# Weight sums of the seven-product blocks: two of four moved from accumulating transfers to VectorE, with shared constant tiles, more raw buffers and new scheduler numbers

## The chip, the core and the metric

The kernel runs on one NeuronCore of a Trainium2 chip. TensorE (PE; its weight loads are listed as PEld), VectorE (DVE), ScalarE (ACT), GpSimd (POOL) and SyncE (SP) each take their instructions in program order and wait for one another through semaphores. SP issues the plain DMA transfers; POOL issues the transfers that add to what lies at their destination. The metric is the device time of one execution in microseconds (us).

## The reference, cut to what matters

Two layers on a residual stream x of 256 tokens by 1024 channels, all float32. Each layer is

```
x += 1/2 * postnorm(SwiGLU(prenorm(x)))        # first feed-forward network (FFN)
x += postnorm(mixer(prenorm(x)))               # S5 state space model + chunk attention, gated
x += 1/2 * postnorm(SwiGLU(prenorm(x)))        # second FFN
def swiglu(h, w_gate, w_up, w_down):
    return (jax.nn.silu(h @ w_gate) * (h @ w_up)) @ w_down     # 1024 -> 2816 -> 1024
```

The S5 part discretises a diagonal complex system with a handful of constant tables that depend on the layer alone (read-out matrices, rotations, decays); the scan over 64-step chunks uses them for both halves of the tokens.

## The kernel before

**Tiles.** The tokens are two tiles t of 128 rows. All weights lie in one array `wall` of 368 chunks of 128 x 1024 float32 (512 KB); a layer has 66 chunks for each FFN and 52 for the mixer, so the FFNs begin at chunks 0, 118, 184 and 302. A chunk is loaded into a buffer of the class `raw`, rounded by ACT to the short matmul format (`wh`, L468), and DVE takes the remainder `raw - wh` (`wl`, L469). With the activations split in the same way, a product of a token tile with half a chunk is three matmuls of 128 x 512 columns: high by high, high by low, low by high (`mm_two_k`, L490, `wide_step`, L508).

**Blocks.** The 2816 hidden columns of an FFN are six blocks b = 0 to 5. Blocks 1 and 3 (`SEVEN`, L31; eight blocks in all) are computed by `seven` (L636): gate and up weights of the block, over two halves of the inner dimension and for two token tiles, are multiplied with seven products in place of eight. A block has twelve chunks i to i+11. Its four weight quadrants are two chunks each: quadrant 11 is i and i+1, quadrant 21 is i+3 and i+4, quadrant 12 is i+5 and i+6, quadrant 22 is i+7 and i+8; i+2, i+9, i+10 and i+11 belong to the down projection of the block before. Products w1 and w2 use quadrants 11 and 21 as they are; w5, w6, w7, w4 use sums of quadrants; w3 uses quadrant 22. The sums are made in place in the `raw` buffers, and each is then converted again by ACT and DVE. `sums` (L610) makes the matching sums of the activations, once for each FFN.

**The four weight sums.** `minus` (L650) negates quadrants 21 and 12 on ACT, and `add` (L654) issues, through `add_to` (L378), an accumulating transfer from POOL for each of the two buffers: 12 into 11 (for w5), 22 into 12 (for w7), 22 into 11 (for w6), 11 into 21 (for w4). That is eight transfers for a block, 64 in all.

**Order.** `Graph` records the operations with a cost, a due time that `take` (L482) and `prod` (L680) derive from `TAU` (L41) times the place in the program, and margins by stream (`MARGIN`, L42). `schedule` (L207) then plays the program with these costs, takes on each engine the operation that can start first (the earliest due among those), and hands out the buffers of `SLOTS` (L37). Each engine's instructions are emitted in the order that comes out. A transfer issued by POOL counts as landed `ADD_LAT` (L54) after its issue. Every matmul, conversion and sum therefore stands in a fixed queue: an instruction that waits holds up all that stand behind it on its engine.

**Constants of S5.** `persistent` (L765) makes `CT`, `D0`, `mt`, `E` (and the two halves of `BT`, L906) in memory of their own, for the whole program; `prep` (L777) fills them once for each layer.

Most instructions of a kind share the line of the helper that records them: L369 is every ACT operation, L376 every DVE tensor-tensor operation, L416 every single matmul, L380 every accumulating transfer, L352 every plain transfer.

Of the kernel before, what the change touches and what calls it, by code (L numbers as in the profile page):

```python
# [12 lines left out]
F32 = mybir.dt.float32  # L13
# [22 lines left out]

SLOTS = {"blk": 28, "ps": 8, "wh": 7, "wl": 7, "raw": 9, "gain": 2,  # L37
         "s1": 16, "s2": 8, "s4": 12, "s16": 8}
ORDERED = ("blk", "ps", "s1", "s2", "s4", "s16", "gain")
LAG = 3  # L40
TAU = 1.355  # L41
MARGIN = {"conv": 7.558, "conv0": 3.423, "task": 7.748, "att0": 37.576, "s50": 37.749, "att1": 28.585, "sums": 8.0, "s51": 29.753, "prep": 40.0}  # L42
PREP_AT = (3, 149)
# [278 lines left out]
class Kern:  # L322
# [84 lines left out]
    def mm(self, out, lhsT, rhs, start, stop, again=False):  # L407
        n, m = rhs.free_size(), lhsT.free_size()
        if rhs.dt == F32R:
            cost = n / 2370  # L410
        elif m == 32:
            cost = 0.05
        else:
            cost = max(0.2, n / 592)
        kw = {"skip_group_check": True} if again else {}
        return self.g.op("pe", cost, [out], [lhsT, rhs], lambda: self.nc.tensor.matmul(  # L416
            out.ap(), lhsT=lhsT.ap(), rhs=rhs.ap(), start=start, stop=stop, **kw))
# [192 lines left out]
    def sums(self, xs):  # L610
# [25 lines left out]
    def seven(self, b, xs, rs, s, acc, pend, first):  # L636
# [127 lines left out]

    def persistent(self):  # L765
        self.CT = [self.own(f"ct{i}", [P, PAIRS, 2, 16], F32) for i in range(4)]
        self.D0 = self.own("d0", [P, 4, P], F32)
        self.S = [self.own(f"st{i}", [P, PAIRS, 65], F32) for i in range(2)]
        for t in self.CT + [self.D0]:
            self.memset("pool", t, 0.0)  # L770
        self.mt = self.own("mt", [P, PAIRS, 64], F32)
        self.memset("pool", self.mt[:, :, 0:1], 0.0)
        self.E = [self.own(f"e{i}", [P, PAIRS, 64], F32) for i in range(2)]
        self.memset("pool", self.E[0][:, :, 0:1], 1.0)
        self.memset("pool", self.E[1][:, :, 0:1], 0.0)
# [173 lines left out]
    def s5(self, t, u):  # L949
# [49 lines left out]
        def rot(h, banks):  # L999
# [306 lines left out]
```

## Time and profile before

| | |
|---|---|
| time, median of 3 runs | 1166.84 us (1166.34 to 1166.95) |
| the profiled execution | 1167.11 us |
| its span, first to last instruction | 1165.3 us |
| busy: PE, PEld, DVE, ACT, POOL | 1131.4, 897.6, 892.3, 696.1, 86.9 us |
| accumulating transfers (queue q0) | 64 of 512 KB, median 7.5 us from issue to landing |
| weight loads | 366 of 512 KB, median 4.6 us |

A PE that is 97% busy is not at its peak everywhere, because a matmul of 512 columns is listed with 401 ns while the next one starts sooner. What counts is where PE sits idle, which engine ends that idle time, and which wait on that engine came before. The profile's line numbers are those of the listing above; times in a window are counted from the first instruction.

### The profile page before, as it was taken

What the parts mean: (1) busy time and instruction counts of PE and PEld (TensorE: products, weight loads), DVE (VectorE), ACT (ScalarE), POOL (GpSimd) and SP (SyncE); (2) the same over time, 40 slices, a digit from 0 to 9 for tenths busy, and PEclk for the clock granted to TensorE, in tenths of its full rate; (3) what the DMA queues carried; (4) which work ended last, traced back from release to release, by engine and by line L of the source; (5) the groups of instructions that cost most, each with busy time, mean ns of one, the idle gap of its engine ahead of it and who ended that gap; (6) DMA issues with size and microseconds to landing.
All of it is one profiled execution on the core that took longest, in us unless ns stands there. A gap on an engine that the chain in (4) does not pass through costs nothing.

```text
span 1165.3 us, 15915 instructions
## 1 busy us (share of the span) xinstructions
PE 1131.4 (97%) x5776; PEld 897.6 (77%) x5776; DVE 892.3 (77%) x1326; ACT 696.1 (60%) x1006; POOL 86.9 (7%) x123
## 2 busy tenths in 40 slices
PE   9889999999999999999999999999999999999997
PEld 7668787877788877878886877778777888778786
DVE  7775997796958887775698659977969589865754
ACT  7746656738654685664476564656485547756542
POOL 3202000100000020200011010000000001102000
PEclk9999999999999999999999999999999999999999
DMA  8988955545264698895669798564533565979831
GB/s 342 233 310 202 340 180 181 171 141 166 66 195 167 207 213 320 193 313 182 199 163 257 271 218 319 163 198 146 175 115 117 161 203 169 231 296 212 321 97 37
DMA packets 69486, 238.60 MB, mean 205 GB/s; under 512 B 8096, under 2 KB 8864, under 8 KB 69408
## 3 DMA queue, kind: packets, MB, share of 16 engines
q1 hardware_dynamic: 60192, 204.03, 50.6%
q0 software_dynamic: 9216, 33.56, 15.7%
q8 instruction: 45, 0.74, 0.3%
q14 instruction: 33, 0.27, 0.1%
HBM read 202.96 MB, written 1.05 MB: 175 GB/s over the span
## 4 chain that ended last, share of the span: by engine, by line
PE 65%; DMA 13%; ACT 8%; DVE 8%; issue 5%; POOL 0%; SPq 0%; POOLq 0%; DVEq 0%; ACTq 0%
PE ps L416 61%; DMA raw<-raw 8%; ACT blk L369 4%; DMA raw<-in_wall_dram 4%; DVE wl L376 4%; ACT wh L369 3%; PE ps L430 3%; DVE blk L376 3%; PE ps L422 1%; DVE blk L1015 1%; POOL raw L380 0%; SPq L352 0%; DVE blk L395 0%; ACT L369 0%; DVE st L376 0%
## 5 line engine op out<-in xcount | busy, mean ns | idle before, releaser
L416 PE MATMUL ps<-wh,blk 128*128 128x512 f32 x2880 | 894.7, 401 | 16.8 <-DVE blk L376 7.5
L376 DVE TENSOR_TENSOR wl<-raw,wh 128x1024 fp32r<-128x1024 f32 (+1 forms) x418 | 500.2, 1217 | 214.6 <-ACT wh L369 212.0
L416 PEld LDWEIGHTS ps<-wh,blk 128*128 128x128 f32 x2880 | 536.7, 189 | 143.5 <-ACT wh L369 13.6
L369 ACT ACTIVATE wh<-raw 128x1024 fp32r<-128x1024 f32 (+1 forms) x418 | 432.7, 1053 | 320.2 <-PE ps L416 234.2
L416 PE MATMUL ps<-wl,blk 128*128 128x512 f32 x1440 | 534.6, 400 | 3.8 <-DVE wl L376 3.8
L416 PEld LDWEIGHTS ps<-wl,blk 128*128 128x128 f32 x1440 | 270.0, 189 | 67.5 <-DVE wl L376 7.3
L369 ACT ACTIVATE blk<-ps 128x512 fp32r<-128x512 f32 (+3 forms) x144 | 81.8, 580 | 87.4 <-PE ps L430 64.4
L376 DVE TENSOR_TENSOR blk<-ps,blk 128x512 fp32r<-128x512 f32 (+2 forms) x144 | 96.1, 671 | 23.3 <-ACT blk L369 22.0
L380 POOL DMA_DIRECT2D raw<-raw x64 | 55.8, 917 | 304.8 <-ACT raw L369 172.5
L430 PE MATMUL ps<-ident,blk 128*128 128x128 f32 x432 | 76.3, 274 | 2.1 <-ACT blk L369 1.2
L430 PEld LDWEIGHTS ps<-ident,blk 128*128 128x128 f32 x432 | 55.8, 140 | 22.2 <-ACT bt L369 2.7
L369 ACT ACTIVATE blk<-ps,s 128x512 f32<-128x512 f32 (+1 forms) x72 | 46.8, 655 | 38.2 <-PE ps L416 37.4
L391 POOL TENSOR_TENSOR s<-s,mhalf 128x1 f32<-128x1 f32 x24 | 22.1, 919 | 549.7 <-DVE s L403 549.7
L369 ACT ACTIVATE blk<-blk 32x128 f32<-32x128 f32 (+3 forms) x132 | 52.2, 396 | 2.5 <-DVE blk L395 0.9
L376 DVE TENSOR_TENSOR blk<-blk,blk 128x512 f32<-128x512 f32 (+3 forms) x70 | 42.5, 626 | 0.2
L369 ACT ACTIVATE blk<-blk,s 128x128 f32<-128x128 f32 (+2 forms) x72 | 31.7, 472 | 8.8 <-DVE blk L376 7.7
L369 ACT ACTIVATE raw<-raw 128x1024 f32<-128x1024 f32 x32 | 33.3, 1051 | 0.2
L395 DVE SCALAR_TENSOR_TENSOR blk<-blk,s,blk 128x512 f32<-128x512 f32 x36 | 26.6, 747 | 2.8 <-ACT blk L369 2.7
L395 DVE SCALAR_TENSOR_TENSOR blk<-ps,s,blk 128x512 f32<-128x512 f32 (+1 forms) x32 | 21.6, 679 | 2.4 <-PE ps L416 1.1
L395 DVE SCALAR_TENSOR_TENSOR blk<-blk,blk 128x512 fp32r<-128x512 f32 (+2 forms) x38 | 21.6, 575 | 0.5 <-ACT blk L369 0.4
L416 PEld LDWEIGHTS ps<-blk,bt 128*128 128x128 f32 x128 | 18.0, 191 | 3.4 <-ACT blk L369 2.1
L376 DVE TENSOR_TENSOR blk<-blk,e 128x512 f32<-128x512 f32 x32 | 20.3, 679 | 0.0
(106 smaller groups left out, 386.8 us busy)
## 6 DMA issues: line engine op xcount, KB each, us to landing
raw<-in_wall_dram SPq DMA_DIRECT2D x366, 512.0 KB, 4.6
raw<-raw POOLq DMA_DIRECT2D x64, 512.0 KB, 7.5
gain<-in_gains_dram SPq DMA_DIRECT2D x22, 256.0 KB, 5.0
blk<-in_bias_dram SPq DMA_DIRECT2D x8, 256.0 KB, 5.0
raw<-in_wall_dram SPq DMA_DIRECT2D x4, 256.0 KB, 4.0
blk<-in_sp_dram SPq DMA_DIRECT2D x4, 256.0 KB, 4.5
x<-in_x_dram SPq DMA_DIRECT2D x3, 256.0 KB, 5.3
out_dram<-x SPq DMA_DIRECT2D x2, 256.0 KB, 2.0
```

Source lines behind the costliest of these rows:

```text
L369: self.nc.scalar.activation(out=out.ap(), in_=in_.ap(), func=func, **k)
L376: lambda: self.nc.vector.tensor_tensor(out=out.ap(), in0=a.ap(), in1=b.ap(), op=op))
L380: lambda: self.nc.gpsimd.dma_start(out=out.ap(), in_=in_.ap(), accum_op=ALU.add), func="dma")
L391: lambda: self.nc.gpsimd.tensor_tensor(out=out.ap(), in0=a.ap(), in1=b.ap(), op=ALU.pow))
L395: return self.g.op("dve", cost, [out], [a, s, b], lambda: self.nc.vector.scalar_tensor_tensor(out=out.ap(), in0=a.ap(), scalar=ap(s), in1= ...
L416: return self.g.op("pe", cost, [out], [lhsT, rhs], lambda: self.nc.tensor.matmul(out.ap(), lhsT=lhsT.ap(), rhs=rhs.ap(), start=start, stop ...
L422: self.nc.tensor.matmul(out.ap(), lhsT=lhsT.ap(), rhs=rhs.ap(), start=start, stop=stop)
L430: lambda o=o, s=s: self.nc.tensor.transpose(o.ap(), s.ap(), self.ident.ap()))
L1015: self.g.op("dve", 0.6, [o], [mt, z], lambda o=o, z=z: self.nc.vector.tensor_tensor_scan(out=o.ap(), data0=mt.ap(), data1=z.ap(), initial= ...
```

## The change

In `seven`, the sums for w5 and w6 (numbers 1 and 2) are made by DVE as a subtraction in place, from quadrant 12 and from quadrant 22; those for w7 and w4 (numbers 3 and 4, `BY_DMA`) stay negations on ACT followed by accumulating transfers. The sum for w5 has the opposite sign, and `sums` has the sign of one activation sum turned to match. `CT` and `D0` are made anew in each layer from the pool of 2 KB `blk` buffers, `mt`, `E` and `BT` from the 4 KB `raw` buffers; the memory that they held goes to the shared classes: `blk` 28 to 33, `raw` 9 to 12, `wh` and `wl` 7 to 8 each. The scheduler's numbers are new: `TAU`, the margin of `sums`, `ADD_LAT` 4.6 to 8.0, the cost of a 512-column matmul 0.216 to 0.232, that of a scan 0.6 to 1.12.

```diff
-SLOTS = {"blk": 28, "ps": 8, "wh": 7, "wl": 7, "raw": 9, "gain": 2,
+SLOTS = {"blk": 33, "ps": 8, "wh": 8, "wl": 8, "raw": 12, "gain": 2,
-TAU = 1.355
-MARGIN = {..., "sums": 8.0, ...}
+TAU = 1.395
+MARGIN = {..., "sums": 3.0, ...}
-ADD_LAT = 4.6
+ADD_LAT = 8.0
+BY_DMA = (3, 4)
...
-            cost = n / 2370
+            cost = 0.0049 + n / 2254
...
-        def add(to, raws):
-            for o, r in zip(to, raws):
-                self.add_to(o, r)
+        def total(k, to, raws):
+            if k in BY_DMA:
+                minus(to)
+                for o, r in zip(to, raws):
+                    self.add_to(o, r)
+            else:
+                for o, r in zip(to, raws):
+                    self.tt(o, r, o, ALU.subtract)
...
-        minus(b21)
         b12 = [self.load(i + 5), self.load(i + 6)]
-        minus(b12)
-        add(b11, b12)
+        total(1, b11, b12)
         w5 = conv(b11)
         b22 = [self.load(i + 7), self.load(i + 8)]
-        add(b12, b22)
-        add(b11, b22)
+        total(3, b12, b22)
+        total(2, b11, b22)
         w6 = conv(b11)
...
-        add(b21, b11)
+        total(4, b21, b11)
...
-    def persistent(self):
-        self.CT = [self.own(f"ct{i}", [P, PAIRS, 2, 16], F32) for i in range(4)]
-        self.D0 = self.own("d0", [P, 4, P], F32)
+    def constants(self, after):
+        self.CT = [tile("blk", PAIRS, 2, 16) for _ in range(4)]
+        self.D0 = tile("blk", 4, P)
...
+        self.mt = tile("raw", PAIRS, 64)
+        self.E = [tile("raw", PAIRS, 64) for _ in range(2)]
...
-            bt = self.own(f"bt{w}", [P, D])
+            bt = self.g.buf("raw", [P, D])
```

What moves on POOL, at the first seven-product block of layer 0's second FFN (i = 126). Here `raw_892` and `raw_893` are quadrant 11, `raw_901` and `raw_902` quadrant 21, `raw_907` and `raw_908` quadrant 12, `raw_913` and `raw_914` quadrant 22; the last number of a name differs from program to program. POOL before, from the pair into quadrant 11 for w5 to the pair into quadrant 21 for w4:

```order
L380 DMA raw_892_3675<-raw_907_3793 128x1024
L380 DMA raw_893_3702<-raw_908_3814 128x1024
L380 DMA raw_907_3793<-raw_913_3854 128x1024
L380 DMA raw_908_3814<-raw_914_3941 128x1024
L380 DMA raw_892_3675<-raw_913_3854 128x1024
L380 DMA raw_893_3702<-raw_914_3941 128x1024
L380 DMA raw_901_3758<-raw_892_3675 128x1024
L380 DMA raw_902_3779<-raw_893_3702 128x1024
```

POOL in the change, the same block with the power operation ahead of it and the next block's first transfer behind it:

```order
L392 TENSOR_TENSOR s1_835_3959<-s1_834_3954,mhalf_2_74 128x1
L381 DMA raw_907_3709<-raw_913_3781 128x1024
L381 DMA raw_908_3730<-raw_914_3795 128x1024
L381 DMA raw_901_3678<-raw_892_3574 128x1024
L381 DMA raw_902_3691<-raw_893_3611 128x1024
L381 DMA raw_1021_4355<-raw_1027_4378 128x1024
```

The four transfers into quadrant 11 are gone, and those into quadrant 21 no longer stand behind two rounds of transfers. DVE before, in the same block, from the conversion of `raw_893` for w5 to that for w6, twelve rows on end; `raw_919` is a chunk of the down projection, names with `blk`, `ps` and `s` are activations:

```order
L376 TENSOR_TENSOR wl_912_4062<-raw_893_3702,wh_911_4046 128x1024
L395 SCALAR_TENSOR_TENSOR blk_872_4073<-ps_874_3970,s1_835_3943,blk_871_3984 128x512
L376 TENSOR_TENSOR blk_878_4001<-blk_881_3947,blk_878_4001 128x512
L376 TENSOR_TENSOR wl_921_4087<-raw_919_4004,wh_920_4058 128x1024
L395 SCALAR_TENSOR_TENSOR blk_885_4099<-blk_878_4001,blk_884_4091 128x512
L376 TENSOR_TENSOR blk_877_4110<-ps_875_4083,blk_876_4095 128x512
L376 TENSOR_TENSOR wl_923_4115<-raw_907_3793,wh_922_4101 128x1024
L395 SCALAR_TENSOR_TENSOR blk_887_4127<-blk_880_3938,blk_886_4032 128x512
L376 TENSOR_TENSOR blk_879_4133<-blk_711_3822,blk_713_3833 128x512
L376 TENSOR_TENSOR wl_925_4141<-raw_908_3814,wh_924_4122 128x1024
L376 TENSOR_TENSOR wl_916_4151<-raw_892_3675,wh_915_4135 128x1024
L376 TENSOR_TENSOR wl_918_4165<-raw_893_3702,wh_917_4145 128x1024
```

DVE in the change, the twelve rows from the second subtraction for w5 to the second one for w6 (`raw<-raw,raw` is a subtraction; quadrant 21's conversions lie between):

```order
L377 TENSOR_TENSOR raw_893_3611<-raw_908_3730,raw_893_3611 128x1024
L377 TENSOR_TENSOR wl_904_4014<-raw_901_3678,wh_903_4002 128x1024
L377 TENSOR_TENSOR blk_870_4024<-ps_868_3992,blk_869_4011 128x512
L377 TENSOR_TENSOR blk_881_3956<-blk_880_3937,blk_881_3956 128x512
L377 TENSOR_TENSOR wl_906_4035<-raw_902_3691,wh_905_4022 128x1024
L377 TENSOR_TENSOR wl_910_4044<-raw_892_3574,wh_909_4032 128x1024
L396 SCALAR_TENSOR_TENSOR blk_883_4055<-blk_881_3956,blk_882_4040 128x512
L377 TENSOR_TENSOR raw_892_3574<-raw_913_3781,raw_892_3574 128x1024
L396 SCALAR_TENSOR_TENSOR blk_872_4071<-ps_874_3985,s1_835_3959,blk_871_3995 128x512
L377 TENSOR_TENSOR wl_912_4079<-raw_893_3611,wh_911_4046 128x1024
L377 TENSOR_TENSOR wl_916_4090<-raw_892_3574,wh_915_4076 128x1024
L377 TENSOR_TENSOR raw_893_3611<-raw_914_3795,raw_893_3611 128x1024
```

Three of the block's four subtractions show here among the conversions; the first, into `raw_892`, stands three rows further up. From the first conversion of `raw_892` to that of the block's last chunk (`raw_937`), DVE has 17 conversions, 4 subtractions and 15 operations of 512 columns in the change, where it had 17 conversions and 15 operations of 512 columns; PE has 123 matmuls of 512 columns there, and had 122. In the first block of all (i = 8), from the conversion of chunk 10 to that of chunk 19, DVE has 15 conversions, 4 subtractions and 12 operations of 512 columns in the change, beside 88 matmuls of 512 columns on PE; it had 13 conversions, 10 operations of 512 columns and 9 small ones beside 84 matmuls.

## Rows read from the trace of the kernel before

**Rows 1.** Waits of PE: engine line, waited for, us in total, times, longest.

```profile
PE ps L416 <- DVE blk L376: 7.5, 6, 4.2
PE ps L416 <- ACT blk L369: 4.8, 8, 2.0
PE ps L416 <- DVE wl L376: 3.8, 7, 0.8
```

**Rows 2.** Busy time by stretch, stretches of the seven-product blocks.

```profile
core 0: us, PE busy (x) PEld busy (x) DVE busy (x) ACT busy (x) POOL busy (x), PEclk, DMA share, GB/s
20.00:76.00 56.00, 48.26 (x202) 37.37 (x201) 43.26 (x64) 35.91 (x44) 10.90 (x9) 0.97 0.99 300
37.00:77.00 40.00, 32.26 (x130) 24.38 (x128) 27.87 (x39) 22.81 (x25) 5.26 (x6) 0.96 1.04 298
128.00:136.00 8.00, 6.93 (x29) 5.08 (x28) 7.86 (x17) 4.06 (x5) 0.00 (x0) 1.00 1.02 405
404.00:447.00 43.00, 41.07 (x182) 32.14 (x181) 37.42 (x47) 32.71 (x40) 8.37 (x10) 1.00 0.86 215
434.00:448.00 14.00, 12.07 (x49) 8.77 (x48) 11.66 (x13) 9.15 (x11) 0.86 (x1) 1.00 0.95 289
455.00:485.00 30.00, 30.00 (x139) 24.32 (x138) 17.54 (x23) 14.55 (x18) 3.50 (x5) 1.00 0.76 225
501.00:517.00 16.00, 13.90 (x52) 10.54 (x52) 15.02 (x19) 11.33 (x13) 0.00 (x0) 0.89 1.01 364
615.00:641.00 26.00, 23.32 (x99) 17.47 (x98) 21.42 (x24) 19.31 (x23) 4.34 (x5) 1.00 0.98 255
694.00:710.00 16.00, 13.88 (x58) 10.43 (x57) 15.86 (x25) 11.16 (x12) 0.00 (x0) 1.00 1.00 371
1000.00:1022.00 22.00, 19.74 (x82) 14.72 (x81) 17.80 (x20) 14.85 (x18) 1.72 (x2) 1.00 1.00 256
1082.00:1086.00 4.00, 3.27 (x14) 2.36 (x13) 3.96 (x6) 2.96 (x4) 0.00 (x0) 1.00 1.02 416
```

**Rows 3.** The chain that ended last: start us, us, what.

```profile
32.85 9.51 DMA raw<-raw
43.19 7.76 DMA raw<-raw
...
53.94 11.40 DMA raw<-raw
...
1149.67 9.06 PE ps L416 x39
```

**Rows 4.** Line L380, the accumulating transfers: issue, waiters, landing.

```profile
L380 POOL DMA_DIRECT2D raw<-raw x64: 862/862/1416, 31.0 to 1072.4; - x64
...
  ACT wh L369: 31.7, 19
...
DMA to landing us min/median/max: 4.5/7.5/11.4
```

**Rows 5.** DVE in order of time: one row near 28 us, then 410 to 447 us.

```profile
27.93 1.22 DVE L376 TENSOR_TENSOR wl<-raw,wh 128x1024 fp32r<-128x1024 f32 x1
...
410.91 2.35 DVE L376 TENSOR_TENSOR wl<-raw,wh 128x1024 fp32r<-128x1024 f32 x2
...
434.70 1.23 DVE L376 TENSOR_TENSOR wl<-raw,wh 128x1024 fp32r<-128x1024 f32 x1 [2.42 <-ACT wh L369]
435.85 0.69 DVE L376 TENSOR_TENSOR blk<-blk,blk 128x512 f32<-128x512 f32 x1
436.45 2.35 DVE L376 TENSOR_TENSOR wl<-raw,wh 128x1024 fp32r<-128x1024 f32 x2
...
443.31 1.23 DVE L376 TENSOR_TENSOR wl<-raw,wh 128x1024 fp32r<-128x1024 f32 x1 [1.64 <-ACT wh L369]
```

**Rows 6.** PE in order of time, near 35 us and near 414 us.

```profile
35.35 0.63 PE L416 MATMUL ps<-wl,blk 128*128 128x512 f32 x2
...
413.97 0.63 PE L416 MATMUL ps<-wl,blk 128*128 128x512 f32 x2
```

More of the change, by code (lines that the diff above doesn't have):

```diff
@@ L40 @@
 LAG = 3
-TAU = 1.355
-MARGIN = {"conv": 7.558, "conv0": 3.423, "task": 7.748, "att0": 37.576, "s50": 37.749, "att1": 28.585, "sums": 8.0, "s51": 29.753, "prep": 40.0}
+TAU = 1.395
+MARGIN = {"conv": 7.558, "conv0": 3.423, "task": 7.748, "att0": 37.576, "s50": 37.749, "att1": 28.585, "sums": 3.0, "s51": 29.753, "prep": 40.0}
 PREP_AT = (3, 149)
@@ L623, in sums @@
         out = []
-        for r, k in ((a22, -1.0), (a11, 1.0), (a21, 1.0), (a12, 1.0)):
+        for r, k in ((a22, 1.0), (a11, 1.0), (a21, 1.0), (a12, 1.0)):
             hi, lo = self.blk(F32R), self.blk(F32R)
@@ L763, in ffn, with tile @@
         return out
-    def persistent(self):
-        self.CT = [self.own(f"ct{i}", [P, PAIRS, 2, 16], F32) for i in range(4)]
-        self.D0 = self.own("d0", [P, 4, P], F32)
-        self.S = [self.own(f"st{i}", [P, PAIRS, 65], F32) for i in range(2)]
-        for t in self.CT + [self.D0]:
[L770 to L775, printed above, removed]
+    def constants(self, after):
+        def tile(cls, *shape):
+            names = "abc"[:len(shape)]
+            t = self.g.buf(cls, [P, math.prod(shape)])
+            return t.rearrange(f"p ({' '.join(names)}) -> p {' '.join(names)}", **dict(zip(names, shape)))
+        self.CT = [tile("blk", PAIRS, 2, 16) for _ in range(4)]
+        self.D0 = tile("blk", 4, P)
+        for t in self.CT + [self.D0]:
+            self.memset("pool", t, 0.0, after)
+        self.mt = tile("raw", PAIRS, 64)
+        self.memset("pool", self.mt[:, :, 0:1], 0.0, after)
+        self.E = [tile("raw", PAIRS, 64) for _ in range(2)]
+        self.memset("pool", self.E[0][:, :, 0:1], 1.0, after)
+        self.memset("pool", self.E[1][:, :, 0:1], 0.0, after)
     def prep(self, l):
@@ L779, in prep @@
         if l == 0:
-            self.persistent()
+            self.S = [self.own(f"st{i}", [P, PAIRS, 65], F32) for i in range(2)]
         after = [self.g.ops[self.mark[(0, PREP_AT[l])]]]
+        self.constants(after)
         prm = self.own("prm", [P, SP_B], F32)
@@ L1014, in rot @@
             for o, z in ((t2, t1), (t4, t3)):
-                self.g.op("dve", 0.6, [o], [mt, z], lambda o=o, z=z: self.nc.vector.tensor_tensor_scan(
+                self.g.op("dve", 1.12, [o], [mt, z], lambda o=o, z=z: self.nc.vector.tensor_tensor_scan(
                     out=o.ap(), data0=mt.ap(), data1=z.ap(), initial=0.0, op0=ALU.mult, op1=ALU.add))
```

## The prediction

> **What bounds the kernel now.** I read the waits of PE first, because an engine that is busy nearly everywhere can only be shortened where it waits. Three pairs make most of its idle time, each ended by DVE or ACT on an activation block or on a freshly converted weight [rows 1]; no transfer stands there as the last cause. The second view is the busy time by stretch, cut where those waits lie: they sit in the eight seven-product blocks. PE's idle time (stretch less PE busy) in the first of the two blocks of each FFN is 7.74, 1.93, 2.68 and 2.26 us, in the second 1.07, 2.10, 2.12 and 0.73 [rows 2] (stretches from 37, 434, 615 and 1000 us, then from 128, 501, 694 and 1082 us): 14.6 + 6.0 = 20.6 us. The third view is the chain of waits, for what lies behind ACT and DVE: in the first block three accumulating transfers follow each other with 9.51, 7.76 and 11.40 us [rows 3]. The fourth is the line of these transfers: 7.5 us in the median, 4.5 to 11.4, and ACT stood still for them 19 times, 31.7 us [rows 4]. The scheduler counts them with 4.6 us, so it puts ACT's next conversion too early into the queue; ACT waits, DVE waits for ACT (2.42 and 1.64 us in one block) [rows 5], and behind that stands the DVE operation that PE needs.
>
> What these stalls cost is more than the idle time. Two matmuls take 0.63 us where one takes 0.40, so the next starts 0.23 us after the one before [rows 6] (39 in 9.06 us: 0.232 [rows 3]), and a listed idle time leaves out 0.40 - 0.23 = 0.17 us of each stall. Some 21 stalls [rows 1] make 3.6 us. The granted clock was 0.96 over the 40 us of the first stretch and 0.89 over the 16 us from 501 [rows 2], worth 0.04 x 40 + 0.11 x 16 = 3.4 us at full speed; both fall after a PE wait, and part of it lies inside the idle time, so I take 2.5. Together the blocks lose 20.6 + 3.6 + 2.5 = 26.7 us. That is all that this change can reach.
>
> **The change part by part.**
>
> *Transfers removed.* 32 of 64 go. They cost no engine time on the path; their price is the waiting. w5 and w6 no longer wait for a transfer at all, and the one into quadrant 21 (w4) can be issued after two subtractions instead of two rounds of transfers (9.51 + 7.76 us in the first block [rows 3]). For w4 in the block at i = 126, between the last subtraction and the conversion of its result the new DVE queue has 8 conversions and 8 operations of 512 columns (8 x 1.15 + 8 x 0.60 = 14 us, spacings from [rows 5]: 434.70 to 435.85, and 435.85 to 436.45). Issue and landing take 0.9 + 7.5 us [rows 4], ACT's rounding about what DVE's conversion takes, 1.2 [rows 5]: 9.6, with the slowest landing 13.5. Both fit.
>
> *Subtractions added.* Four for each block, 32 in all, at DVE's spacing for 128 x 1024, 1.15 us: 4.6 us a block, 36.8 in all. They have the form of the conversion's own subtraction, so this price needs no bound. Whether PE feels it depends on DVE's lead.
>
> In second blocks it has one: DVE is busy 17.54 of 30 us ahead of the stall at 501 [rows 2], and the stall comes because ACT's waits push its work together. With the waits gone 9 us (two blocks' sums) would fit into such a stretch. I leave 0.5 us for the four together; bound 6.0 (nothing gained) plus their share of the rest.
>
> In first blocks it has almost none, since the activation sums and the end of the norm fall there too. By the order, from the first conversion of the block at i = 126 to that of its last chunk, DVE has 21 operations of 1.15 and 15 of 0.60 us: 33.2 us. PE has 123 x 0.232 = 28.5. DVE falls behind by 4.7 us; before it was 17 x 1.15 + 15 x 0.60 = 28.6 against 28.3, almost even. What covers this is the lead with which DVE enters: its conversion ended at 412.1 (first of the two at 410.91) and PE read it at 414.20 (second of the pair at 413.97) [rows 5, 6], 2.1 us. The eighth `wh`/`wl` pair lets it enter earlier by at most about one half-chunk product of two tiles, 12 x 0.232 = 2.8 us. So this block keeps a stall of 0 (full lead) to 2.6 us (lead as traced); I take 2.0, nearer to the traced lead. The first blocks from 615 and 1000 us have the same queue: 2.0 each.
>
> In the very first block DVE has 19 x 1.15 + 12 x 0.60 = 29.1 us from chunk 10 to chunk 19, PE 88 x 0.232 = 20.4: behind by 8.7. Its lead there was 35.35 - 29.15 = 6.2 [rows 5, 6]. That leaves 2.5, and with half a us of waiting for ACT in a queue without slack 3.0; bounds 0 and 8.7.
>
> *Order and buffers.* The negation of quadrant 12 now stands behind the subtraction that reads it, on ACT's queue with the conversions behind it. Between that subtraction and the conversion for w7 stand 10 operations of 1.15 and 8 of 0.60 us, 16.3 in all, against the negation's 1.2 and the 9.6 above: 0. If that cover went, each first block would pay the slowest landing's 3.9 us more, less the slack of 5.5: still 0. Three more `raw` buffers let loads run ahead; the constants take three of them back from chunk 3 on, and two more in `prep`, until the mixer ends, so first FFNs have 9 as before and second FFNs 12. POOL clears the constants once for each layer: 8 more clears on an engine that loses half its transfers, 0. In the mixers the number of PE switches to small matmuls falls by some ten; I count 0, and bound it by the 0.23 us of a matmul each, -2.3 to +2.3.
>
> *The sum.* Left in the blocks: 3.0 + 3 x 2.0 + 0.5 = 9.5 us of 26.7, so 17.2 us are gained. Against the profiled execution's 1167.1 us (0.3 above the median) this is **1149.9 us**.
>
> *A rule that speaks against it.* The transfers measured 4.5 to 11.4 us [rows 4]. The Trainium skill, "DMA: Bandwidth & Descriptors", section "Anatomy of one DMA — SWDGE (gpsimd) path", gives a transfer issued by GpSimd 2.0 us plus its bytes over 436e3, an estimate of 3.2 us for 512 KB. By that rule they land sooner than the scheduler counts, nobody waits for them, and the time would stay at 1167. The trace does not agree: its fastest is 4.5 us.
>
> **The rivals.**
>
> *A. DVE takes over as the bound in first blocks, chance 0.10.* Place: DVE's queue between w2 and w6. It is idle 5.6 of the 43 us from 404 [rows 2] (6.1 and 6.0 in the two like it). If these waits are not the transfers' but ACT's own lateness, they stay, and the 4.6 us of each of four first blocks come on top of the old stalls: +18.4. The second blocks still gain their 6.0 idle + 1.5 hidden + 1.5 clock - 0.5 = 8.5. 1167.1 + 9.9 = 1177. It decides at a DVE idle time above 43 - 37.4 - 4.6 = 1.0 us in that stretch. For it: the 4.7 us by which DVE falls behind. Against: both long waits in [rows 5] end with a conversion that waited for a transfer, and the first block has 12.7 us of DVE idle time in the stretch from 20 us [rows 2].
>
> *B. First blocks only swap the cause, 0.15.* PE waits as long as before, for DVE instead of the transfers; only the second blocks gain: 1167.1 - 8.5 = 1158.6.
>
> *C. The transfers are hidden anyway, 0.05.* DVE's lateness has another cause, such as the small operations of `prep`. 1167. Against: 31.7 us of ACT waiting [rows 4].
>
> *D. The constants starve the loads, 0.05.* Nine, then seven `raw` buffers hold a block that needs eight at once; first FFNs gain nothing. The second FFNs gain their 1.93 + 2.10 + 2.26 + 0.73 = 7.0 less 4.5 left, plus 1.8 of clock: 1163. Against: 9 were enough before, and `BT` is made after the blocks.
>
> **How the numbers follow.** The forecast has 0.65. Its own range is 1140 (all 26.7 us gone) to 1158 (B's edge). The range of 8 in 10 takes in B and D: 1140 to 1164; A and C, 0.15, and a little below stay out. Within 0.2% (2.3 us, about what a measurement tells from no change) is 1164.5 to 1169.2: C and an edge of D, 0.07. Slower: A and what the new queues could bring that I don't see, 0.11. Faster: 0.82.
>
> **What would show it.** In the profile after: 32 transfers on POOL, ACT's waits for them down from 31.7 us to under 5; 32 DVE subtractions `raw<-raw` of 1.2 us; no PE wait over 1 us in second blocks; DVE over 95% busy in first blocks, PE waits there ended by DVE `wl`; the granted clock at 1.00 through 501 to 517. Wrong would be: ACT still waiting for transfers (the slack that I counted is not there), PE waits of over 3 us behind DVE in first blocks (A), or new waits for `in_wall_dram` (D).

## The result, and the profile after

The changed kernel takes 1151.82 us (median of four runs, 1150.75 to 1153.01) where the kernel before takes 1166.89 beside it: a ratio of 0.9871, 95% interval 0.9854 to 0.9888. That is 15.1 us less; 17.2 were predicted. The profiled execution took 1152.82 us, its span is 1151.0. Several medians of before stand in this text (1166.9 to 1167.5), since each set of runs had its own beside it.

First what the sums did. The page, part 1 (busy us, share, instructions) and two groups of part 5:

```profile
PE 1128.7 (98%) x5776; PEld 897.9 (78%) x5776; DVE 919.3 (80%) x1358; ACT 695.0 (60%) x1006; POOL 64.3 (6%) x99
...
L381 POOL DMA_DIRECT2D raw<-raw x32 | 27.8, 870 | 288.2 <-ACT raw L370 233.8
L377 DVE TENSOR_TENSOR raw<-raw,raw 128x1024 f32<-128x1024 f32 x32 | 38.8, 1223 | 0.3
```

The 32 subtractions cost DVE 38.8 us and are there with 1.22 us each. The line of the transfers, as in [rows 4]:

```profile
L381 POOL DMA_DIRECT2D raw<-raw x32: 859/860/1030, 35.7 to 1054.8; - x32
...
who waited for it (us, times):
...
DMA to landing us min/median/max: 4.5/5.6/9.5
```

No engine waits for a transfer any more; ACT had stood still for 31.7 us [rows 4]. SP, which issues the loads, still waits for them for 2.3 us, after 52.9 in the kernel before. The waits of PE, as in [rows 1], without those of the first 11 us and one of 0.2 us:

```profile
PE ps L431 <- ACT raw L370: 4.1, 2, 2.3
PE ps L417 <- ACT blk L370: 4.0, 5, 1.8
PE ps L423 <- ACT blk L370: 2.2, 2, 1.1
...
PE ps L417 <- DVE blk L402: 0.8, 1, 0.8
PE ps L417 <- DVE blk L377: 0.6, 2, 0.4
PE ps L417 <- DVE wl L377: 0.2, 1, 0.2
```

The waits of the large matmuls (L417) for `blk` and `wl` of DVE, 7.5 and 3.8 us before [rows 1], are down to 1.4 and 0.2. On top stand waits for ACT now: L431 is a transpose, L423 a small matmul of the mixer. None of those three rows lies in a block. The stretches show where they lie. The rows of after (columns as in [rows 2]) are cut at points of TensorE's own work, so that they hold the same matmuls as the rows of before below them: the start, the first block at i = 8, mixer 0, the first blocks at i = 126 and 192, mixer 1.

```profile
0.00:30.17 30.17, 25.00 (x104) 19.30 (x105) 19.17 (x35) 20.94 (x38) 5.30 (x14) 0.94 0.88 331
30.17:74.80 44.63, 44.41 (x196) 35.36 (x194) 44.62 (x61) 32.96 (x38) 3.64 (x4) 1.00 0.92 298
152.41:326.10 173.69, 168.92 (x1131) 130.64 (x1130) 138.50 (x221) 106.98 (x208) 5.18 (x14) 1.00 0.46 154
426.41:466.34 39.93, 39.93 (x176) 32.14 (x175) 32.95 (x37) 23.67 (x27) 0.25 (x1) 1.00 0.84 292
606.53:636.72 30.19, 30.19 (x133) 24.31 (x132) 30.19 (x33) 21.97 (x25) 1.72 (x2) 1.00 0.89 289
722.33:941.74 219.41, 215.20 (x1333) 168.47 (x1332) 169.49 (x253) 129.43 (x234) 4.95 (x12) 0.99 0.47 162
```

The kernel before, the same six pieces of work:

```profile
0.00:26.13 26.13, 23.26 (x105) 18.64 (x106) 18.21 (x35) 18.63 (x36) 10.77 (x19) 1.00 0.90 343
26.13:80.76 54.63, 46.89 (x195) 36.29 (x194) 42.02 (x65) 33.88 (x40) 7.17 (x8) 0.97 0.98 292
158.23:327.66 169.43, 167.52 (x1131) 130.21 (x1129) 142.58 (x231) 107.00 (x207) 6.13 (x14) 1.00 0.47 152
427.91:470.77 42.86, 40.93 (x175) 32.05 (x174) 30.70 (x33) 23.70 (x27) 1.72 (x2) 1.00 0.88 287
614.99:649.08 34.09, 31.41 (x134) 24.03 (x132) 29.35 (x31) 24.62 (x28) 4.34 (x5) 1.00 0.99 291
736.98:951.65 214.67, 212.76 (x1334) 166.90 (x1332) 172.30 (x262) 130.41 (x235) 5.76 (x12) 1.00 0.49 157
```

The block at i = 8 is 10.0 us shorter, those at 126 and 192 are 2.9 and 3.9 shorter and PE has no idle time left in them. But the start takes 4.0 us longer, mixer 0 4.3, mixer 1 4.7. For the rest of this text I count the loss of a stretch: its length less what its matmuls take at the pace of undisturbed stretches (0.232 us for 512 columns, 0.108 for a transpose, 0.050 for a small one; 1102.4 us in all). The start is counted from 1.2 us on, since TensorE's first matmul begins at 1.4 us in every run.

| lost, us | start | eight blocks | mixer 0 | mixer 1 | median, us |
|---|---|---|---|---|---|
| before | 4.8 | 30.7 | 9.4 | 9.7 | 1166.9 |
| after | 8.8 | 2.9 | 13.7 | 14.4 | 1151.8 |

The blocks gave 27.8 us, and the start and the mixers took 13.0 of them back. Below, "first blocks" are the first seven-product block of each FFN (i = 8, 126, 192, 310), "second blocks" the other four (32, 150, 216, 334).

### The profile page after: what moved, and what is told of

The parts are those of the page before. It is cut to its first block, busy times and chain, and to the rows that moved or that the text cites. A ratio compares the mean times of both kernels' runs of the same rounds, so it can differ in the third digit from the quotient of the medians.

```text
span 1151.0 us, 15872 instructions
## 1 busy us (share of the span) xinstructions
PE 1128.7 (98%) x5776; PEld 897.9 (78%) x5776; DVE 919.3 (80%) x1358; ACT 695.0 (60%) x1006; POOL 64.3 (6%) x99
## 4 chain that ended last, share of the span: by engine, by line
PE 85%; ACT 5%; DVE 4%; issue 3%; DMA 2%; POOL 0%; SPq 0%; DVEq 0%; ACTq 0%; POOLq 0%
PE ps L417 80%; PE ps L431 4%; DVE wl L377 2%; ACT blk L370 2%; ACT wh L370 2%; DMA raw<-in_wall_dram 1%; PE ps L423 1%; DVE blk L377 1%; DVE blk L396 1%; DMA x<-in_x_dram 0%; ACT raw L370 0%; POOL s L392 0%; DVE raw L377 0%; SPq L353 0%; ACT L370 0%
## 5 line engine op out<-in xcount | busy, mean ns | idle before, releaser
L417 PE MATMUL ps<-wh,blk 128*128 128x512 f32 x2880 | 893.5, 401 | 3.2 <-ACT blk L370 1.8
L417 PEld LDWEIGHTS ps<-wh,blk 128*128 128x128 f32 x2880 | 537.7, 189 | 128.6 <-ACT blk L370 3.8
L377 DVE TENSOR_TENSOR wl<-raw,wh 128x1024 fp32r<-128x1024 f32 (+1 forms) x418 | 498.6, 1218 | 168.4 <-ACT wh L370 165.8
L370 ACT ACTIVATE wh<-raw 128x1024 fp32r<-128x1024 f32 (+1 forms) x418 | 433.1, 1053 | 299.3 <-PE ps L417 248.8
L417 PE MATMUL ps<-wl,blk 128*128 128x512 f32 x1440 | 531.9, 399 | 0.2 <-DVE wl L377 0.2
L417 PEld LDWEIGHTS ps<-wl,blk 128*128 128x128 f32 x1440 | 270.7, 189 | 63.0 <-DVE wl L377 1.8
L370 ACT ACTIVATE blk<-ps 128x512 fp32r<-128x512 f32 (+4 forms) x152 | 84.0, 562 | 76.3 <-PE ps L431 55.6
L377 DVE TENSOR_TENSOR blk<-ps,blk 128x512 fp32r<-128x512 f32 (+2 forms) x144 | 95.8, 672 | 9.5 <-ACT blk L370 9.2
L431 PE MATMUL ps<-ident,blk 128*128 128x128 f32 x432 | 82.6, 276 | 4.3 <-ACT raw L370 4.1
L431 PEld LDWEIGHTS ps<-ident,blk 128*128 128x128 f32 x432 | 55.9, 140 | 22.6 <-ACT raw L370 4.8
L370 ACT ACTIVATE blk<-blk 32x128 f32<-32x128 f32 (+4 forms) x148 | 58.8, 399 | 22.9 <-DVE blk L377 14.7
L370 ACT ACTIVATE blk<-ps,s 128x512 f32<-128x512 f32 (+1 forms) x72 | 46.4, 656 | 27.8 <-PE ps L417 21.6
L381 POOL DMA_DIRECT2D raw<-raw x32 | 27.8, 870 | 288.2 <-ACT raw L370 233.8
L377 DVE TENSOR_TENSOR blk<-blk,blk 128x512 f32<-128x512 f32 (+3 forms) x70 | 42.9, 629 | 0.1
L370 ACT ACTIVATE blk<-blk,s 128x128 f32<-128x128 f32 (+2 forms) x72 | 31.8, 473 | 15.9 <-DVE blk L377 15.8
L377 DVE TENSOR_TENSOR raw<-raw,raw 128x1024 f32<-128x1024 f32 x32 | 38.8, 1223 | 0.3
L370 ACT ACTIVATE raw<-raw 128x1024 f32<-128x1024 f32 x32 | 33.7, 1055 | 2.9 <-DVE raw L377 2.9
L396 DVE SCALAR_TENSOR_TENSOR blk<-blk,s,blk 128x512 f32<-128x512 f32 x36 | 26.7, 748 | 2.6 <-ACT blk L370 2.4
L377 DVE TENSOR_TENSOR blk<-ps,raw 128x512 f32<-128x512 f32 x32 | 19.8, 682 | 6.8 <-PE ps L417 6.8
L417 PEld LDWEIGHTS ps<-blk,blk 128*32 128x32 f32 (+2 forms) x256 | 15.4, 147 | 12.1 <-issue 9.8
```

What stands on the lines that cost most here:

```text
L370: self.nc.scalar.activation(out=out.ap(), in_=in_.ap(), func=func, **k)
L377: lambda: self.nc.vector.tensor_tensor(out=out.ap(), in0=a.ap(), in1=b.ap(), op=op))
L381: lambda: self.nc.gpsimd.dma_start(out=out.ap(), in_=in_.ap(), accum_op=ALU.add), func="dma")
L396: return self.g.op("dve", cost, [out], [a, s, b], lambda: self.nc.vector.scalar_tensor_tensor(out=out.ap(), in0=a.ap(), scalar=ap(s), in1= ...
L431: lambda o=o, s=s: self.nc.tensor.transpose(o.ap(), s.ap(), self.ident.ap()))
```

## The experiments

The names of lines are those of the kernel after (L370 ACT, L377 DVE, L417 PE's large matmuls); in the kernel before and in the first experiment they are one lower.

**The numbers alone** (before with the five new scheduler numbers).

```diff
-TAU = 1.355        "sums": 8.0   ADD_LAT = 4.6   n / 2370            scan 0.6
+TAU = 1.395        "sums": 3.0   ADD_LAT = 8.0   0.0049 + n / 2254   scan 1.12
```

> The kernel before with the new scheduler numbers alone (TAU, margin of sums, ADD_LAT 8.0, matmul and scan costs); all four sums stay transfers, constants and buffers as before. Theory A (the gain comes from taking the transfers for w5 and w6 off the path; a true landing time in the plan cannot shorten the three transfers in a row of 9.5, 7.8 and 11.4 us): about a third of the gain, 1158 to 1163 us, PE stalls left in all first blocks. Rival B (the plan's wrong landing time was the whole fault): 1152. If the mixers lose their 9 us and the start its 4 us here too, the numbers are their cause; if not, the shared constants are.

Measured 1185.13 us (1180.65 to 1188.61), 1.0154 of before (1.0126 to 1.0183): slower by 18 us, and both expectations missed. PE now waits for freshly converted weights most of all:

```profile
PE ps L416 <- ACT wh L369: 13.9, 7, 5.3
```

ACT waits for weight loads instead of transfers. The transfers, counted with 8.0 us now, keep it 2.4 us (31.7 in [rows 4]), the loads 45.8 (19.2 in the kernel before):

```profile
ACT wh L369 <- DMA raw<-in_wall_dram: 45.8, 24, 6.9
...
ACT wh L369 <- DMA raw<-raw: 2.4, 4, 1.0
```

The blocks lose 31.9 us, no less than before, and the mixers 13.5 and 13.6: their loss in the kernel after is here without any other part of the change. The start loses 5.2, so its 8.8 in the kernel after need the numbers together with another part. Some 7 us more than before are lost between the stretches of the table.

**All four sums by transfer** (after).

```diff
-BY_DMA = (3, 4)
+BY_DMA = (1, 2, 3, 4)
```

> The change with all four sums by transfers (BY_DMA = 1, 2, 3, 4; quadrant 11 is negated on ACT twice for it, 4 more ACT operations of 1.05 us a block), memory and scheduler numbers as in the change. Theory A: the transfers in a row are back on the path, 1159 to 1164 us, the loss lying in the first blocks, most in the very first. Rival C (the eighth pair and the twelve raw buffers made the gain): 1152 to 1153.

1165.42 us (1162.91 to 1168.9), ratio 0.9987 (0.9976 to 0.9998): the gain is gone, a little further than theory A said. The longest wait is in the block at i = 8 (time, us, and in brackets the engine's idle time and what ended it), first on PE and then on ACT:

```profile
60.32 2.17 PE L417 MATMUL ps<-wh,blk 128*128 128x512 f32 x4 [4.41 <-ACT wh L370]
```

```profile
59.21 2.95 ACT L370 ACTIVATE wh<-raw 128x1024 fp32r<-128x1024 f32 x3 [4.87 <-DMA raw<-in_wall_dram]
```

ACT waits for a weight load there, not for a transfer. In the profiled execution (1162.91 us) the blocks lose 11.6 us, 8.6 of them at i = 8; three lose between 0.6 and 1.6 and the other four at most 0.1, though two waits of PE, of 1.5 and 2.4 us, lie just ahead of the stretches at 150 and 216. So with the new numbers and memory a good half of the blocks' 30.7 us goes even with all transfers left, but the start (9.0) and the mixers (12.3 and 11.6) take much of that back, and little is gained over before. The time with the subtractions is 13.6 us lower, which speaks against the rival by which the transfers were hidden anyway. What the memory alone does beside the old numbers and all eight transfers was not run.

**All four sums on DVE** (after).

```diff
-BY_DMA = (3, 4)
+BY_DMA = ()
```

> The change with all four sums on VectorE (BY_DMA empty): 32 more subtractions of 1.15 us spacing, no transfers from GpSimd, no negations on ACT. Theory A with VectorE's lead as the limit of first blocks: by the order DVE falls 3.6 to 4.9 us further behind than its buffers allow in each of the four first blocks (chunks 18, 137, 203, 321), so PE waits there 3 to 5 us each, ended by DVE wl: 1162 to 1170. Rival (first blocks have spare room, as their waits of under 0.4 us in the change suggest): 1150 to 1153.

1155.17 us (1154.65 to 1155.53), ratio 0.9899 (0.9885 to 0.9914). The first blocks lose 5.1, 3.2, 5.0 and 3.4 us, as expected; of the 9.8 us that PE stands idle in them 5.5 are ended by DVE and the rest by ACT. The waits of the whole program:

```profile
PE ps L417 <- ACT blk L370: 7.7, 9, 1.8
PE ps L417 <- DVE wl L377: 5.2, 6, 1.6
```

Two more sums on DVE are too many for a first block. The total came out 7 us under the expectation because the mixers lose 8.3 and 8.9 here instead of 13.7 and 14.4, though no instruction of theirs was touched. That was the first sign that their loss is a matter of the order.

**Constants in memory of their own** (after with the slots, `constants` and `BT` of before).

```diff
-SLOTS = {"blk": 33, ..., "wh": 8, "wl": 8, "raw": 12, ...}
+SLOTS = {"blk": 28, ..., "wh": 7, "wl": 7, "raw": 9, ...}
...
-            t = self.g.buf(cls, [P, math.prod(shape)])
+            t = self.own(..., [P, math.prod(shape)])
```

> The change without its memory part: constants in memory of their own, 28 blk, 9 raw, 7 wh and 7 wl buffers as before; sums and scheduler numbers as in the change. Theory A: the blocks keep nearly all of their gain, 1 to 2 us of stalls come back in the first blocks of chunks 8 and 192. Rival C: most of the gain goes, 1160 or more. For the mixers: if the shared constants cost them the 9 us, this kernel is at 1144 to 1147; if the scheduler numbers do, at 1151 to 1155.

1153.43 us (1152.94 to 1154.23), ratio 0.9883 (0.9867 to 0.99). Beside the new numbers the memory is worth 1.6 us. That is a balance: the blocks lose 9.3 us here where after loses 2.9, and the mixers 11.6 and 11.8 where after loses 13.7 and 14.4. Theory A holds in that most of the blocks' gain stays, but what comes back is in second blocks (6.8 us) more than in first ones (2.6).

**All five old numbers** (after).

```diff
-TAU = 1.395        "sums": 3.0   ADD_LAT = 8.0   0.0049 + n / 2254   scan 1.12
+TAU = 1.355        "sums": 8.0   ADD_LAT = 4.6   n / 2370            scan 0.6
```

> The kernel after with all five scheduler numbers of the kernel before (TAU 1.355, sums margin 8.0, ADD_LAT 4.6, 2,370 columns per us, scan 0.6). The new kernel loses 8.8 us over TensorE's pace in its start (4.8 in the kernel before) and 13.7 and 14.3 us in its mixers (9.4 and 9.6). Theory N, the numbers do that through the order: the start goes back to 4.8 and the mixers to about 10.5 each, the blocks stay within 1 us, in all about 10.5 us less than after: 1,141 us. Theory M, the start is the numbers' work but the mixers' loss is the shared constants': 1,148 us. Theory K, the numbers are needed for the blocks (planned with 4.6 us for a transfer, w4's conversion comes too early): each of eight blocks loses 1.5 us or more, so 1,153 us or above.

1138.22 us (1138.02 to 1138.35), ratio 0.9744 (0.9731 to 0.9757): 13.6 us faster than after. Theory N holds for the start (5.6 us) and is exceeded in the mixers (5.4 us each). Its condition that the blocks stay within 1 us of after does not hold. Rows of the same work as above, mixer 0 and mixer 1:

```profile
149.19:314.56 165.37, 164.67 (x1131) 129.87 (x1130) 141.95 (x231) 107.55 (x209) 5.19 (x14) 1.00 0.51 164
...
714.28:924.74 210.46, 209.72 (x1334) 166.53 (x1333) 171.94 (x261) 129.94 (x235) 4.95 (x12) 1.00 0.52 169
```

The mixers are 8.3 and 9.0 us shorter than after. The blocks lose 8.7 us for 2.9: the first ones 2.2, 1.8, 2.2 and 2.1 us, behind DVE (4.4 us in 8 waits), where after loses 0.8 in all four. So the new numbers do help, by 7.5 us in first blocks, and cost 20.5 in the start and the mixers.

**One number at a time** (after with one or two put back).

```diff
-                self.g.op("dve", 1.12, [o], [mt, z], ...
+                self.g.op("dve", 0.6, [o], [mt, z], ...
```

> The kernel after with the scan's planned duration alone put back (1.12 to 0.6). The order ahead of the first mixer's s50 chain is the same in both, so the start's 8.8 us stay. Theory S, the longer scan pushes the s5 chain back in the order and makes the waits of the mixers at 227 to 276 and 793 to 842 us (0.6 + 0.9 + 1.3 us in each): both mixers lose about 2.8 us less, 1,146 us. Theory P, it is the pace (TAU and the matmul's cost): no change, 1,151 to 1,152.5 us with those waits still there.

```diff
-TAU = 1.395              cost = 0.0049 + n / 2254
+TAU = 1.355              cost = n / 2370
```

> The kernel after with TAU and the matmul's cost alone put back (1.355, 2,370 columns per us); sums margin, transfer latency and scan stay new. In the order ScalarE's copy of the feed-forward's first result at the start now stands behind the two normalised pieces of tile 1, as in the kernel before; in the kernel after it stands ahead of them and of three conversions. Theory P, the pace sets the start and the mixers: start back to 4.8 us, mixers to about 10.5 each, 1,141 us. Theory S, it sets the start alone and the scan the mixers: 1,148 us. Theory O, the wait of 2.0 us at 22.02 us and the 2 us around it come by something else than that copy's place: 1,151 us or more.

The scan alone gives 1143.47 us (1141.52 to 1146.81), theory S and a little more; the mixers lose 10.2 and 9.6. The old pace gives 1137.31 (1136.33 to 1138.71), theory P and more: the start loses 5.5, the mixers 6.1 and 6.4. What happened in the start can be read on ACT. After, in order of time:

```profile
15.55 2.01 ACT L370 ACTIVATE wh<-raw 128x1024 fp32r<-128x1024 f32 x2
20.08 0.69 ACT L370 ACTIVATE blk<-ps,s 128x512 f32<-128x512 f32 x1 [2.52 <-POOL s L392]
20.66 1.05 ACT L370 ACTIVATE wh<-raw 128x1024 fp32r<-128x1024 f32 x1
21.61 0.62 ACT L370 ACTIVATE blk<-ps,gcol 128x128 fp32r<-128x128 f32 x2
```

With the old pace:

```profile
19.50 2.03 ACT L370 ACTIVATE wh<-raw 128x1024 fp32r<-128x1024 f32 x2
21.39 0.38 ACT L370 ACTIVATE blk<-ps,gcol 128x128 fp32r<-128x128 f32 x1
21.64 1.08 ACT L370 ACTIVATE wh<-raw 128x1024 fp32r<-128x1024 f32 x1
22.59 0.39 ACT L370 ACTIVATE blk<-ps,gcol 128x128 fp32r<-128x128 f32 x1
22.84 0.72 ACT L370 ACTIVATE blk<-ps,s 128x512 f32<-128x512 f32 x1
```

`blk<-ps,s` needs a small number from POOL that is not there before 20 us. After, it stands at the head of ACT's queue and holds up three conversions and the pieces of tile 1's first norm (`blk<-ps,gcol`) for 2.52 us; with the old pace it stands behind them and waits for nothing. PE after reads those pieces:

```profile
22.02 0.50 PE L417 MATMUL ps<-wh,blk 128*128 128x512 f32 x1 [1.81 <-ACT blk L370]
```

The mixers after show the same figure: ACT waits 3.16 us for DVE, behind it stands a copy into `BT`, and PE's transposes wait 2.25 us for the buffer of that copy.

```profile
175.88 0.84 ACT L370 ACTIVATE blk<-blk 64x256 f32<-64x256 f32 x2 [3.16 <-DVE blk L377]
177.01 0.60 ACT L370 ACTIVATE raw<-ps 128x512 f32<-128x512 f32 x1 [0.29 <-DVE wl L377]
```

```profile
177.66 0.66 PE L431 MATMUL ps<-ident,blk 128*128 128x128 f32 x4 [2.25 <-ACT raw L370]
```

**BT in memory of its own** (after).

```diff
-SLOTS = {..., "raw": 12, ...}
+SLOTS = {..., "raw": 10, ...}
-            bt = self.g.buf("raw", [P, D])
+            bt = self.own(f"bt{w}", [P, D])
```

> The kernel after with BT's two tiles in memory of their own and 10 raw tiles for 12, the memory that they take. In the new kernel the transposes of the preparation wait 2.4 us (177.66) and 2.0 us (742.16) for ScalarE's copy into BT, which is a raw tile. Theory B, the raw tile is the reason: both waits go, 4.4 us less, 1,147.5 us if 10 raw tiles do for the blocks. Theory R, the copies are late by their place in ScalarE's queue, whatever tile they fill: the waits stay, and 10 raw tiles for 12 cost up to the 1.6 us that the memory part was worth: 1,152 to 1,153.5 us.

1162.99 us (1162.08 to 1165.81), ratio 0.9962 (0.9948 to 0.9976), outside both expectations. The mixers lose 10.6 and 10.8, about 3 less each, and the wait for the copy is gone; but the order is another one, so this does not show that the shared tile was its reason. The blocks at i = 8, 32, 192 and 216 lose 6.9, 2.8, 7.2 and 3.2 us; those at 126, 150, 310 and 334 lose nothing, as after. The first four run while the constants hold three `raw` tiles (requested at chunks 3 and 149 and kept to the end of each mixer), and so have 7 of 10 in place of 9 of 12. The block at 150 has 7 as well, since POOL clears those tiles at 493.5 to 498.9 us and its stretch begins at 499.7; so 7 were too few in four of five blocks. (The prediction gave all second FFNs 12; the block at 150 has 9 in the kernel after.) ACT's waits for weight loads rise from 9.1 us in the kernel after to 38.1, of which 32.7 lie in and around the four blocks that lose. This is the rival of the starved loads, which the change escaped by two tiles; how much of each block's loss goes through those waits is not settled, since with fewer tiles the whole order is another.

**The sums alone** (before with the sums of after; old memory, all old numbers). The kernel is made from after with the rest put back, so its lines are those of after, and the constants are still cleared once for each layer.

```diff
+BY_DMA = (3, 4)
...
+        def total(k, to, raws): ...
```

> The kernel before with nothing but the sums changed: two of four as subtractions on VectorE, constants and BT in memory of their own, the old numbers of slots (28 blk, 9 raw, 7 wh, 7 wl) and all five old scheduler numbers. Theory S, the sums are the gain: with the old numbers the first blocks lose 2 us each behind VectorE, as in the run with old numbers (2.2, 1.8, 2.2, 2.1), the second blocks under 0.5, the start 5.6; the mixers 5.5 to 9.5: 1,138 to 1,146 us. Theory M, memory and sums are both needed (nine raw tiles hold the sums' operands back): the blocks lose 3 us or more each as in the kernel before, 1,150 us or above.

1155.09 us (1154.21 to 1156.12), ratio 0.9895 (0.9881 to 0.9908). The sums by themselves take the transfers off ACT's path, with the old 4.6 us in the plan (31.7 us in [rows 4]):

```profile
ACT wh L370 <- DMA raw<-raw: 1.1, 2, 0.8
```

The blocks lose 18.7 for 30.7, start and mixers stay (5.2, 9.8, 10.0). Theory M is right that the memory is needed for the rest, though not by 3 us in each block: the first blocks lose 7.0, 3.6, 3.3 and 3.2, the second 1.8 together. PE's longest wait is again the block at i = 8, where ACT waited 2.11 us for a load:

```profile
57.57 0.80 PE L417 MATMUL ps<-wh,blk 128*128 128x512 f32 x1 [3.82 <-ACT wh L370]
```

With this run two of four sums on DVE have been timed in all four combinations, and all sums by transfer in three:

| us | two sums on DVE, old numbers | two on DVE, new numbers | all by transfer, old numbers | all by transfer, new numbers |
|---|---|---|---|---|
| constants of their own | 1155.1 | 1153.4 | 1166.9 | 1185.1 |
| shared constants, more slots | 1138.2 | 1151.8 | not run | 1165.4 |

The sums are worth 11.8 us beside the old memory and numbers, 31.7 beside the old memory and new numbers, and 13.6 beside both new ones. With the sums on DVE, the memory is worth 16.9 us beside the old numbers and 1.6 beside the new; the numbers are worth 1.7 beside the old memory and cost 13.6 beside the new.

**TAU, the scan and the rest** (after).

```diff
-TAU = 1.395
+TAU = 1.355
```

> The kernel after with TAU alone put back (1.395 to 1.355); the matmul's cost stays new. In the order the copy of the feed-forward's first result still stands ahead of tile 1's pieces on ScalarE, so the wait at 22 us and the start's 8.8 us stay. Theory T, TAU sets the mixers: they lose 6 to 10 us each for 13.7 and 14.3, about 1,141 us. Theory C, the matmul's cost does, and TAU does little: 1,150 to 1,153 us.

Next, TAU, the matmul's cost and the scan put back together:

> The kernel after with TAU, the matmul's cost and the scan put back; the sums' margin (3.0) and a transfer's planned time (8.0) stay new. Theory L, these two are what shortens the first blocks (1.2 to 1.7 us lost in the run with the old pace, 1.8 to 2.2 with all old numbers): first blocks 1.5 us or less each, mixers 5.5 each, 1,136 us. Theory N, they do nothing: first blocks 2 us each, 1,138 us.

And last, when these two had been timed, TAU and the scan without the matmul's cost:

> The kernel after with TAU (1.355) and the scan's planned duration (0.6) put back; the matmul's cost, the sums' margin and a transfer's planned time stay new. In the run with TAU alone the first blocks lose 0 to 0.6 us, where they lose 1.2 to 1.7 with the matmul's cost put back as well; the start loses 7.6 and the mixers 9.3 and 8.5. Theory A, the gains add: the scan takes from the mixers what it took at the new TAU (3.5 and 4.8 us), the first blocks stay under 0.6 and the start at 7.6: 1,132 us, under the best so far (1,135.3). Theory B, they do not add, since one order serves for both: the mixers stay above 8 us, 1,138 us or more.

TAU alone: 1140.58 us (1140.22 to 1141.29); start 7.6, mixers 9.3 and 8.5, first blocks 0.6 in all. Theory T. TAU, matmul and scan: 1135.29 us (1134.5 to 1135.82), ratio 0.9724 (0.9711 to 0.9737), the fastest kernel here and nearer to theory L, with start 5.2, first blocks 1.2 to 1.7 and mixers 4.9 and 5.4. TAU and scan without the matmul's cost: 1142.71 us (1140.22 to 1144.61), theory B; the scan that took 8 us off the kernel after takes nothing off here (1140.58 without it, and the ranges overlap). The gains of single numbers do not add.

Two pairs of these runs differ in the matmul's planned cost alone, and it is what sets the first blocks:

| lost, us | start | first blocks | second blocks | mixers | median, us |
|---|---|---|---|---|---|
| old TAU, new cost | 7.6 | 0.6 | 1.6 | 17.8 | 1140.6 |
| old TAU, old cost | 5.5 | 6.0 | 0.6 | 12.5 | 1137.3 |
| old TAU and scan, new cost | 7.5 | 0.7 | 1.5 | 20.0 | 1142.7 |
| old TAU and scan, old cost | 5.2 | 6.0 | 0.6 | 10.3 | 1135.3 |

The new cost saves 5.3 to 5.4 us in the first blocks and costs about 2 in the start, 1 in the second blocks and 5.3 to 9.7 in the mixers.

## Why the prediction was right, and where it was not

The total was 2 us off, and that is luck: two steps were wrong by far more, with opposite signs. The blocks gained 27.8 us where 17.2 were said (2.9 of 30.7 are left, not 9.5 of 26.7), and the start and the mixers cost 13.0 where nothing was said.

*Transfers off the path: right.* ACT no longer waits for them, no PE wait over 1 us is left in second blocks (the longest is 0.8), and the clock that was 0.89 [rows 2] is 1.00 there:

```profile
495.00:510.00 15.00, 15.00 (x67) 12.15 (x66) 14.83 (x27) 9.79 (x10) 0.13 (x1) 1.00 0.83 311
```

The run of the sums alone shows that the sums do this and gain by it: ACT's waits for transfers fall from 31.7 to 1.1 us and the time by 11.8. That ACT stops waiting for transfers is not enough, though. The numbers alone do that too (2.4 us left), and there ACT waits for loads and the time rises. Second blocks keep 2.1 us, 0.5 were said.

*The price of a subtraction: right.* 1.22 us by the page against 1.15 by spacing, and DVE is full in first blocks as foretold, 42.98 us of 43 where it had 37.42 [rows 2]:

```profile
404.00:447.00 43.00, 43.00 (x192) 34.73 (x191) 42.98 (x51) 34.21 (x42) 6.61 (x5) 1.00 0.74 222
```

*What is left in first blocks, 3.0 + 3 x 2.0 us: mis-sized.* Measured 0.8 in all four. The term hangs on DVE's lead, and I kept near the 2.1 us of [rows 5, 6]. The lead after is 4.2 us; the conversion of chunk 126 ends at 407.66 + 1.22 = 408.88, PE reads it at 413.11:

```profile
407.66 1.22 DVE L377 TENSOR_TENSOR wl<-raw,wh 128x1024 fp32r<-128x1024 f32 x1
```

```profile
413.11 0.48 PE L417 MATMUL ps<-wl,blk 128*128 128x512 f32 x1
```

The upper bound of the prediction, 2.1 + 2.8 = 4.9, was the better value of the lead. It comes with the eighth `wh`/`wl` pair: in the four kernels with seven pairs the lead at this place is 1.4 to 2.9 us, in the ten with eight it is 4.2 to 4.8. But the lead does not decide what is left. The run with old numbers and the new memory has 4.4 and loses 2 us in this block. The run with constants in memory of their own has 1.4 (the conversion ends at 408.59 + 1.22 = 409.81, and PE reads it as the second of the pair at 411.01, at 411.24) and loses nothing here:

```profile
408.59 2.35 DVE L377 TENSOR_TENSOR wl<-raw,wh 128x1024 fp32r<-128x1024 f32 x2
```

```profile
411.01 0.63 PE L417 MATMUL ps<-wl,blk 128*128 128x512 f32 x2
```

With the lead as it came, the prediction's own sum leaves 4.7 - 4.2 = 0.5 us in this block, near what was measured; in those two runs the same sum would leave 0.3 and 3.3, where 2 and nothing came. So two things failed: the lead was taken too short, and it is not only the lead that covers the 4.7 us by which DVE was to fall behind. The order inside the block decides, and of the numbers it is the matmul's planned cost that sets it (with two sums on DVE and the full new memory, 6.0 to 8.3 us are left in first blocks with the old cost, 0.6 to 0.8 with the new one); which instructions it moves is not settled.

*Order, buffers and mixers, 0 with 2.3 either way: wrong.* They cost 13.0 us. I had bounded the mixers by the number of switches between large and small matmuls; what came are waits of 0.3 to 2.3 us behind ACT's queue, and the start was not in the sum at all. The cause is the new scheduler numbers: the run with all old ones loses 3.2 us less in the start and 17.3 less in the mixers. In the mixers the numbers do it alone (13.5 and 13.6 in the first experiment), though not with every set of operations: with all sums on DVE the same numbers leave 8.3 and 8.9. In the start they need the new sums or the new memory beside them: 5.2 with neither, 8.9 with the sums, 9.0 with the memory. What happens there is shown (the copy that stands too early, PE's wait of 1.81 us behind it, and the clock after that). In the mixers only the largest waits are; why truer durations give them a worse order stays open. That the numbers were read off a trace was no reason to cost them at nothing.

*The rivals.* DVE as the bound is what the run with all sums on DVE begins to show, at 1155 us and not 1177. Swapped causes in first blocks: not seen after, 2 us a block with old numbers. Transfers hidden anyway: excluded by the run of the sums alone, which is 11.8 us faster than before. Starved loads: not here, but two `raw` tiles away. Not excluded is that the memory alone would have gained much beside the old numbers, since that kernel was not run with all sums by transfer.

## What to carry to other kernels

When a planner's numbers change, cost every stretch that it orders, also those that no edited line touches: look in each engine's new queue for an instruction that waits for another engine and now stands ahead of work that does not. Time new durations apart from the change that they come with, one by one and in pairs, since their gains do not add; here the better measured ones cost 13.6 us, and old TAU, matmul and scan with new margin and transfer time gave 1135.3. And when an engine gets more work in a stretch, take its lead from the new number of buffers and not from the old trace, and do not take the lead for all that decides: here a block with 1.4 us of lead lost nothing and one with 4.4 lost 2.

## What the runs showed of the hardware

The clock did not answer to every wait alike. After PE's wait of 1.81 us at 22.02 it was granted at half speed, 1.2 GHz, for 3.4 us in all (0.37 x 2 + 0.48 x 2 = 1.7 us of clock are missing from the 4 us below), and after one of 1.86 us at 742.16, in mixer 1, for as long. After the 2.25 us at 177.66, in mixer 0, it stayed at 2.4 GHz. Kernel after:

```profile
22.00:24.00 2.00, 1.98 (x6) 1.56 (x7) 2.00 (x3) 2.00 (x3) 0.00 (x0) 0.63 1.00 399
24.00:26.00 2.00, 2.00 (x7) 1.56 (x5) 1.57 (x4) 2.00 (x5) 0.55 (x1) 0.52 1.05 420
...
178.00:180.00 2.00, 2.00 (x12) 1.65 (x11) 0.53 (x2) 1.63 (x4) 0.00 (x0) 1.00 0.00 0
```

```profile
744.00:746.00 2.00, 2.00 (x6) 1.52 (x5) 1.23 (x1) 1.22 (x2) 0.00 (x0) 0.50 0.00 0
```

Even the same wait had both outcomes. The run with `BT` in memory of its own has PE wait 1.82 us at 22.07 for the same copy, and the clock stays up:

```profile
22.00:24.00 2.00, 1.93 (x8) 1.61 (x9) 2.00 (x3) 2.00 (x4) 0.00 (x0) 1.00 0.79 315
```

That gives the price. From this wait to the end of the start PE has the same 28 matmuls of 512 columns in both, with no further wait. They take 8.15 us in the kernel after (8.16 to 8.20 in three other runs whose clock fell there) and 6.91 in this run (6.90 in the one with all sums on DVE, whose clock stayed up too). So 1.2 of the 4.0 us that the start lost are the clock.

The accumulating transfers landed sooner where there were fewer: median 7.5 us with 64 in the kernel before [rows 4], 7.9 and 6.5 in two other runs with 64, 5.6 with 32 in the kernel after and 5.1 to 6.6 in other runs with 32; the fastest was 4.5 us each time. The two ranges touch, so their number is not all that counts.
